# Moving convolutions and operand sums within VectorE's order in a two-layer decoder trunk

## The chip, the cores and the metric

The kernel runs on one core of a Trainium2 chip. Time is device time in microseconds of one execution, the median of three runs. The core's engines work side by side, each through its own instructions in a fixed order: TensorE (PE; PEld is its weight load), VectorE (DVE), ScalarE (ACT), GpSimd (POOL), and SyncE (SP), which here only issues loads. An instruction that waits holds up everything behind it on its engine.

## The reference, cut to what matters

A trunk of two layers over 256 tokens of width 2048: a gated linear attention layer, then an attention layer that reads a shared K/V, each followed by a gated feed-forward part with a convolution. The change touches the feed-forward parts:

```python
def conv_ffn(x, norm_w, w_up, conv_w, conv_b, w_down):
    h = rms_norm(x, norm_w) @ w_up                # (256, 2 * 5632)
    hp = jnp.pad(h, ((0, 0), (CONV_WIDTH - 1, 0), (0, 0)))
    acc = conv_b
    for j in range(CONV_WIDTH):                   # 3 taps back in time
        acc = acc + conv_w[j] * hp[:, j:j + S]
    a, u = jnp.split(acc, 2, axis=-1)
    return (jax.nn.silu(a) * u) @ w_down          # (256, 2048)
```

All is float32, and every matrix product is as exact as that asks for.

## The kernel before

**Weight pieces.** Weights are read once, in raw tiles of 128 x 2048 (three buffers, `wraw`, loaded by SyncE at L96). Each tile is used in pieces of 1024 columns or fewer. For each piece ScalarE rounds a high part (`whi`, L140) and VectorE subtracts it to get the low part (`wlo`, L141); three TensorE products of high and low parts (of weights and of activations, split likewise) give one product in full precision. High and low pieces have three buffers each, with some every fourth piece in a larger pool, so both engines work only a few pieces ahead of TensorE. `step()` marks the passing of one piece; `after(n, job)` puts a job n pieces later in the program. A tile scheduler then fixes each engine's order; it may pull an instruction forward unless `issue_after` ties it behind another. `ws.behind()` ties what stands in its scope behind the casts of the latest piece.

**Up-projection.** `ffn` goes through 22 groups J of 8 pieces. Each group's result is transposed, stored and fetched in another layout (`store`, `load`, GpSimd's queue, into `upT`), and later `convolve` (L670 to L689) makes two column blocks j of the hidden activations `hid`: on ScalarE L676 twice, L684 and L303, on VectorE L680 twice, L682 twice, L685 and L304. Group J's two convolutions were due 7 and 9 pieces after its group ends, so group 20's fell into group 21 and into the start of the down projection, and group 21's into its places 6 and 1+.

**Down projection.** `down` goes twice (b = 0, 1; half of the output columns each) through the 22 pairs of hidden blocks, in an order written by hand: for `dn0`, and for the first half of `dn1`, `0 2 4 6 1+ 8 3+ 10 5+ 12 7+ 14 9+ 16 11+ 17 13+ 18 15+ | 19 20 21` (in `dn0`'s second half 19 stands ahead of the bar). I call each entry a place. A plain place has two pieces and 24 matmuls (8 products). A place with a plus ("seven") gets along with seven products, 21 matmuls in four pieces, for sums of operands: VectorE makes sums of the raw weights (`t`, L106 to L108) and splits them too, and the activations' sums `comb` come from `combine` (L603 to L606, then a split at L303 and L304). Pairs 1, 3, 5, 7 are summed during the up-projection (`EARLY`); 9, 11, 13, 15, and 17 in the second half of `dn1`, by `combine_parts` (L613, then `combine`), written two places ahead of use, but with nothing that ties them there. The places behind the bar, the tail, are gone through twice, once for each half of the columns; behind the body's last seven place, L754 to L758 join the seven products and GpSimd adds the residual from memory (L760), and L769 adds the tail's sums.

Of the kernel before, what the change touches and what calls it, by code (L numbers as in the profile page):

```python
# [27 lines left out]
FT = F // 128  # L28
# [9 lines left out]
def _order(text):  # L38
# [3 lines left out]


EARLY = (1, 3, 5, 7)
ORDERS = {
    "go": [_order("0 1+ 2 3+ 4 | 5 6 7"), _order("0 2 1+ 3+ 4 | 5 6 7")],
    "dn0": [_order("0 2 4 6 1+ 8 3+ 10 5+ 12 7+ 14 9+ 16 11+ 17 13+ 18 15+ | 19 20 21"),
# [110 lines left out]
def trunk(ctx: ExitStack, tc: tile.TileContext, xT, x_tok, cst, msk, w1p, w2a, w_k, w_qa, w_v2, w_v, w_g, w_go,  # L158
# [27 lines left out]
    ws = WeightStream(tc, raw, parts)  # L186
# [4 lines left out]
    for w, groups, cols in plan:  # L191
        if cols is None:
            for g, order in enumerate(ORDERS[groups]):
                ws.add_quads(w, g, order, groups in ("go", "mo"))
# [74 lines left out]
    def after(steps, job):  # L269
        later.append((cur[0] + steps, job))  # L270
# [28 lines left out]
    def rows(xs):  # L299
        return lambda kt: xs[kt // 2][:, kt % 2, :]  # L300
# [54 lines left out]
    xs = rows(nrm.xs)  # L355
# [255 lines left out]
    def combine_parts(k, xs, into):  # L611
        t = temp("whole")
        V.tensor_add(t, xs[k][:, :, :S], xs[k][:, :, S:])  # L613
        combine(k, [(t[:, i, :128], t[:, i, 128:]) for i in range(2)], into)

    def sevens(name):
        return {k for order, _ in ORDERS[name] for k, seven in order if seven}

# [25 lines left out]
    def ffn(layer, nrm, then):  # L644
        xs = rows(nrm.xs)
        hid, sums = [], {}
        whole = [None, None]
        cw = C_CW + layer * 3 * 2 * FT
        cb = C_CB + layer * 2 * FT
        turned = dram.tile([FT // 2, 16, 32, 4, 64], F32, name=f"turned{layer}")  # L650

        def square(ps):
            z = slot([128, 16, 2, 32], F32, "z")
            for t in range(2):
                tok = temp("tok", (128, 512))
                A.activation(tok, ps[:, t, :], AF.Copy, scale=nrm.woven[:, t:t + 1])
                V.transpose(z[:, :, t, :], tok.rearrange("p (a b) -> p a b", b=32))  # L657
            return z

        def store(J, z):  # L660
            nc.gpsimd.dma_start(turned[J].rearrange("(a i) r q c -> (i r) a (q c)", a=4),  # L661
                              z.rearrange("p (a q) t c -> p a (q t c)", a=4))

        def load(J):
            f = slot([128, 4, S], F32, "upT")
            for q in range(4):
                nc.gpsimd.dma_start(f[32 * q:32 * q + 32].rearrange("p a (i c) -> p (a i) c", i=4),  # L667
                                  turned[J][:, :, q, :].rearrange("a r c -> r a c"))
            return f

        def convolve(j, t):
            au = temp("au")
            with ws.behind():
                for i in range(2):
                    n = i * FT + j
                    A.activation(au[:, i, :], t[:, i, :], AF.Identity, bias=col(cb + n),  # L676
                                 scale=col(cw + 2 * 2 * FT + n))
            for i in range(2):
                n = i * FT + j
                V.scalar_tensor_tensor(au[:, i, 1:], t[:, i, :S - 1], col(cw + 2 * FT + n), au[:, i, 1:],  # L680
                                       op0=OP.mult, op1=OP.add)
                V.scalar_tensor_tensor(au[:, i, 2:], t[:, i, :S - 2], col(cw + n), au[:, i, 2:],  # L682
                                       op0=OP.mult, op1=OP.add)
            A.activation(au[:, 0, :], au[:, 0, :], AF.Silu)  # L684
            V.tensor_mul(au[:, 0, :], au[:, 0, :], au[:, 1, :])  # L685
            if j % 2 == 0:
                hid.append(slot([128, 2, 2 * S], F32R, "hid"))
            split(hid[-1][:, j % 2, :S], hid[-1][:, j % 2, S:], au[:, 0, :])
            whole[j % 2] = (au[:, 0, :128], au[:, 0, 128:])  # L689
            if j % 2 and j // 2 in EARLY:  # L690
                combine(j // 2, whole, sums)

        f = {}
        for J in range(FT // 2):
            z = gemm_tok(xs, 1, square)
            after(1, lambda J=J, z=z: store(J, z))
            after(2, lambda J=J: f.update({J: load(J)}))
            for i in range(2):
                after(7 + 2 * i, lambda J=J, i=i: convolve(2 * J + i, f[J][:, 2 * i:2 * i + 2, :]))
        then(hid, sums)  # L700

    def down(name, xs, combos, res, done, jobs):

        for b, (order, n_tail) in enumerate(ORDERS[name]):
            new = [k for k, seven in order if seven and k not in combos]
            todo = {i: list(js) for i, js in jobs.get(b, {}).items()}
            for k in new:
                at = next(i for i, (k_, _) in enumerate(order) if k_ == k)
                todo.setdefault(max(at - 2, 0), []).append(lambda k=k: combine_parts(k, xs, combos))
            low = acc_ps.tile([128, 2, 512], F32, name="acc")  # L710
            p = {2: low[:, 0], 3: low[:, 1], 4: bank("p4", (128, 512)), 8: bank("p8", (128, 512))}
            left = dict.fromkeys(range(1, 9), 0)
            for k, seven in order:
                for n in ((1, 5, 7, 6, 4, 3, 2) if seven else (2, 3, 4, 8, 2, 3, 4, 8)):
                    left[n] += 3
            begun = set()

            def prods(*todo):

                w = step()  # L720
                for n, _, _ in todo:
                    if n not in p:
                        two = acc_ps.tile([128, 2, 512], F32, name="acc")
                        p.update({n: two[:, 0], {1: 6, 5: 7}[n]: two[:, 1]})
                for xi, wi in ((0, 0), (1, 0), (0, 1)):
                    for n, x, f in todo:
                        left[n] -= 1
                        T.matmul(p[n], x[xi], w[wi][:, 512 * f:512 * f + 512], start=n not in begun, stop=left[n] == 0)  # L728
                        begun.add(n)

            def part(k, i, t):
                x = xs[k][:, i, 128 * t:]
                return x[:, :128], x[:, S:S + 128]

            def comb(k, f):
                return combos[k][:, f, 0], combos[k][:, f, 1]

            last = max(i for i, (k, seven) in enumerate(order) if seven)
            for i, (k, seven) in enumerate(order[:-n_tail]):
                for job in todo.get(i, ()):  # L740
                    job()
                if seven:
                    prods((1, part(k, 0, 0), 0))
                    prods((3, comb(k, 3), 0), (2, part(k, 1, 0), 1))
                    prods((5, comb(k, 0), 0), (7, comb(k, 2), 1))
                    prods((6, comb(k, 1), 0), (4, part(k, 1, 1), 1))
                else:
                    for a in range(2):
                        prods(*((n, part(k, a, t), f)
                                for n, t, f in ((2, 0, a), (3, 0, 1 - a), (4, 1, a), (8, 1, 1 - a))))  # L750
                if i == last:

                    r = [temp(f"c{n}", (128, 512)) for n in range(4)]
                    A.copy(r[0], p[1])  # L754
                    V.tensor_add(r[1], r[0], p[6])  # L755
                    V.tensor_add(r[2], r[1], p[7])
                    V.tensor_add(r[1], r[1], p[5])
                    V.tensor_add(r[3], r[2], p[5])  # L758
                    for n in (0, 2, 1, 3):
                        nc.gpsimd.dma_start(r[n], res(n // 2, 2 * b + n % 2), accum_op=OP.add)  # L760
            for f, ns in enumerate(((2, 4), (3, 8))):
                for i, (k, _) in enumerate(order[-n_tail:]):
                    for job in todo.get((f, i), ()):
                        job()
                    prods(*((n, part(k, a, t), a) for a in range(2) for t, n in enumerate(ns)))
                if f:
                    ws.prefetch(cur[0])
                for t, n in enumerate(ns):
                    V.tensor_add(r[2 * t + f], r[2 * t + f], p[n])  # L769
                    done(t, 2 * b + f, r[2 * t + f])  # L770
# [212 lines left out]
    xs = rows(n_q.xs)  # L983
    for g in range(4):
# [4 lines left out]
        f = (q8[:, g % 2 * 4:g % 2 * 4 + 4], (q1[:, 0:2], q1[:, 2:4]))  # L989
        qf.append(f)  # L990
        head_through(g, z, [(11, lambda x, f=f: features(x, f, 1.0, 1))])
    xs = rows(xkv)
    for g in range(4):
# [3 lines left out]
        f = (k8[:, g % 2 * 4:g % 2 * 4 + 4], [slot([128, 2, 2, S], F32R, f"k1{c}") for c in range(2)])  # L997
# [120 lines left out]
```

## Time and profile before

| | us |
|---|---|
| runs (device time) | 2194.74, 2199.5, 2194.8; median 2194.8 |
| profiled execution, device time | 2194.64 |
| its span, first to last instruction | 2192.9 |
| mean granted TensorE clock | 0.998 |
| up-projection of layer 1 ends, body of `dn0` begins | 866.42 |
| tail of `dn0`'s first half begins | 969.24 |
| body of `dn1` begins, its tail begins | 1954.61, 2057.02 |

How to read it: busy times are sums over an engine's instructions within the span; the chain that ended last is followed back from the last instruction to whatever released it. The averages cover stages with different limits, so each stage has to be read from its own stretch.

### The profile page before, as it was taken

Reading aid. Unit: us, or ns where it says so; the run is one execution under the profiler, and the core shown is the slowest. Engines: PE = TensorE matmul, PEld = TensorE weight load, DVE = VectorE, ACT = ScalarE, POOL = GpSimd, SP = SyncE. Lnnn points to the kernel's source line nnn. Section 1 sums busy time; section 2 is a strip of 40 time slices with the busy share of each in tenths; the row PEclk is TensorE's granted clock in tenths of the full one; section 3 lists DMA queues with packets and bytes.
Section 4 is the critical chain, followed back from the end, with each engine's and each line's share of the span. In section 5 each row is a group of like instructions: output and inputs, shape, how many; then the busy total and the mean of one; then the engine's idle time right before and its main releaser. Section 6 shows DMA issues by size and latency. Waiting matters only on the chain.

```text
span 2192.9 us, 26952 instructions
## 1 busy us (share of the span) xinstructions
PE 2171.7 (99%) x9693; PEld 1793.4 (82%) x9693; DVE 1593.7 (73%) x2190; ACT 1283.0 (59%) x1856; POOL 301.1 (14%) x448
## 2 busy tenths in 40 slices
PE   9999999999999999999999999999999999999999
PEld 7888887888888888788888888888888888887887
DVE  5655586667776767887857787676777676779886
ACT  6545665556565656556556676555656565556554
POOL 1011111111111111000013242011111111110000
PEclk9999999999999999999999999999999999999999
DMA  8465577576777777566577787576677777774655
GB/s 306 177 234 208 186 244 251 206 247 230 239 249 249 241 239 242 180 235 237 210 258 261 271 279 229 205 235 230 233 248 237 248 235 249 236 242 186 231 209 173
DMA packets 92104, 510.11 MB, mean 233 GB/s; under 512 B 13713, under 2 KB 14753, under 8 KB 41922
## 3 DMA queue, kind: packets, MB, share of 16 engines
q1 hardware_dynamic: 60578, 417.53, 53.9%
q0 software_dynamic: 30816, 90.28, 15.3%
q8 instruction: 76, 1.25, 0.2%
q10 hardware_dynamic: 576, 0.58, 0.1%
q14 instruction: 58, 0.48, 0.1%
HBM read 463.22 MB, written 45.11 MB: 232 GB/s over the span
## 4 chain that ended last, share of the span: by engine, by line
PE 86%; issue 10%; DMA 3%; DVE 1%; ACT 0%; POOL 0%; SPq 0%; ACTq 0%; POOLq 0%; DVEq 0%
PE acc L290 45%; PE acc L293 22%; PE acc L728 10%; PE p L728 6%; DMA wraw<-w_go 1%; DMA c<-rows 1%; ACT whi L140 0%; PE sT L561 0%; PE o L578 0%; DMA wraw<-w_v 0%; DVE wlo L141 0%; PE acc L793 0%; PE s L910 0%; POOL upT L667 0%; DMA gn<-cst 0%
## 5 line engine op out<-in xcount | busy, mean ns | idle before, releaser
L141 DVE TENSOR_TENSOR wlo<-wraw,whi 128x1024 fp32r<-128x1024 f32 (+1 forms) x786 | 930.0, 1191 | 423.2 <-ACT whi L140 401.1
L140 ACT CAST whi<-wraw 128x1024 fp32r<-128x1024 f32 (+1 forms) x786 | 798.6, 1026 | 639.7 <-PE acc L290 415.8
L290 PE MATMUL acc<-whi,xw 128*128 128x512 f32 x3840 | 953.6, 390 | 3.5 <-ACT whi L140 2.6
L290 PEld LDWEIGHTS acc<-whi,xw 128*128 128x128 f32 x3840 | 720.7, 188 | 154.8 <-ACT whi L140 3.0
L293 PE MATMUL acc<-wlo,xw 128*128 128x512 f32 x1920 | 514.5, 389 | 0.0
L293 PEld LDWEIGHTS acc<-wlo,xw 128*128 128x128 f32 x1920 | 360.2, 188 | 74.9
L728 PE MATMUL acc<-whi,hid 128*128 128x512 f32 x572 | 182.5, 391 | 3.6 <-DVE c L769 2.2
L728 PE MATMUL p<-whi,hid 128*128 128x512 f32 x506 | 166.3, 390 | 0.0
L667 POOL DMA_DIRECT2D upT<-turned x176 | 114.0, 654 | 147.8 <-DMA turned<-z 60.1
L140 ACT CAST whi<-t 128x1024 fp32r<-128x1024 f32 x82 | 85.5, 1051 | 77.1 <-PE p L728 43.3
L728 PEld LDWEIGHTS acc<-whi,hid 128*128 128x128 f32 x572 | 106.8, 188 | 27.7 <-DVE c L769 3.0
L290 PE MATMUL acc<-whi,xkv 128*128 128x512 f32 x512 | 128.8, 391 | 0.0
L661 POOL DMA_DIRECT2D turned<-z x44 | 34.0, 774 | 677.2 <-DVE z L657 614.8
L676 ACT ACTIVATE au<-upT,cs 128x256 f32<-128x256 f32 x176 | 96.0, 595 | 52.4 <-DMA upT<-turned 52.3
L728 PE MATMUL acc<-whi,comb 128*128 128x512 f32 x328 | 108.2, 394 | 5.7 <-ACT whi L140 5.6
L728 PEld LDWEIGHTS p<-whi,hid 128*128 128x128 f32 x506 | 94.8, 188 | 19.8
L290 PEld LDWEIGHTS acc<-whi,xkv 128*128 128x128 f32 x512 | 94.6, 188 | 18.7
L680 DVE SCALAR_TENSOR_TENSOR au<-upT,cs,au 128x255 f32<-128x255 f32 x176 | 77.2, 472 | 41.7 <-ACT au L676 41.6
L141 DVE TENSOR_TENSOR wlo<-t,whi 128x1024 fp32r<-128x1024 f32 x82 | 99.1, 1219 | 5.4 <-ACT whi L140 3.9
L728 PE MATMUL acc<-wlo,hid 128*128 128x512 f32 x286 | 94.8, 390 | 2.0 <-DVE wlo L141 2.0
L760 POOL DMA_DIRECT2D c<-rows x24 | 21.2, 1052 | 466.9 <-DVE c L755 454.9
L728 PE MATMUL p<-wlo,hid 128*128 128x512 f32 x253 | 83.6, 389 | 0.0
(251 smaller groups left out, 1950.5 us busy)
## 6 DMA issues: line engine op xcount, KB each, us to landing
wraw<-w_up SPq DMA_DIRECT2D x176, 1024.0 KB, 5.3
wraw<-w_dn SPq DMA_DIRECT2D x88, 1024.0 KB, 5.0
turned<-z POOLq DMA_DIRECT2D x44, 512.0 KB, 3.5
upT<-turned POOLq DMA_DIRECT2D x176, 128.0 KB, 4.9
wraw<-w_g SPq DMA_DIRECT2D x16, 1024.0 KB, 4.9
wraw<-w_go SPq DMA_DIRECT2D x16, 1024.0 KB, 6.3
wraw<-w_mq SPq DMA_DIRECT2D x16, 1024.0 KB, 5.3
wraw<-w_kk SPq DMA_DIRECT2D x16, 1024.0 KB, 6.2
```

The lines of the kernel that those rows point to most:

```text
L140: one = nc.scalar.copy(hi[:, a:b], src[:, a:b])
L141: two = nc.vector.tensor_sub(lo[:, a:b], src[:, a:b], hi[:, a:b].bitcast(F32))
L290: T.matmul(ps[:, t, :], xs(kt)[:, x0 + 128 * t:x0 + 128 * t + 128], hi[:, c:c + 512], start=kt == 0 and x0 == 0, stop=False)
L293: T.matmul(ps[:, t, :], xs(kt)[:, 128 * t:128 * t + 128], lo[:, c:c + 512], start=False, stop=kt == KT - 1)
L661: nc.gpsimd.dma_start(turned[J].rearrange("(a i) r q c -> (i r) a (q c)", a=4), z.rearrange("p (a q) t c -> p a (q t c)", a=4))
L667: nc.gpsimd.dma_start(f[32 * q:32 * q + 32].rearrange("p a (i c) -> p (a i) c", i=4), turned[J][:, :, q, :].rearrange("a r c -> r a c"))
L676: A.activation(au[:, i, :], t[:, i, :], AF.Identity, bias=col(cb + n), scale=col(cw + 2 * 2 * FT + n))
L680: V.scalar_tensor_tensor(au[:, i, 1:], t[:, i, :S - 1], col(cw + 2 * FT + n), au[:, i, 1:], op0=OP.mult, op1=OP.add)
L728: T.matmul(p[n], x[xi], w[wi][:, 512 * f:512 * f + 512], start=n not in begun, stop=left[n] == 0)
L760: nc.gpsimd.dma_start(r[n], res(n // 2, 2 * b + n % 2), accum_op=OP.add)
```

## The change

The four convolutions of the last two groups of each up-projection (J = 20, 21) are due 24 pieces later, at pieces 23, 25, 31 and 33 of the down projection: in its order at places 5+, 12, 14 and 9+. And `combine_parts` is now issued behind the latest piece's casts at the place where it is written, so that the scheduler can't pull the sums forward.

```diff
+LAST = (FT // 2 - 2, FT // 2 - 1)
...
             for i in range(2):
-                after(7 + 2 * i, lambda J=J, i=i: convolve(2 * J + i, f[J][:, 2 * i:2 * i + 2, :]))
+                after(7 + 2 * i + (24 if J in LAST else 0),
+                      lambda J=J, i=i: convolve(2 * J + i, f[J][:, 2 * i:2 * i + 2, :]))
...
     def down(name, xs, combos, res, done, jobs):
+
+        def parts_behind(k):
+            with ws.behind():
+                combine_parts(k, xs, combos)
...
-                todo.setdefault(max(at - 2, 0), []).append(lambda k=k: combine_parts(k, xs, combos))
+                todo.setdefault(max(at - 2, 0), []).append(lambda k=k: parts_behind(k))
```

The added lines move line numbers: L106, L141, L304, L603, L613 and L680 of before are L107, L142, L305, L604, L614 and L681 after, and L728 is L734. The orders of GpSimd and SyncE are the same before and after; ScalarE's moves with VectorE's.

VectorE before, at place 1+ of `dn0` (`t_7040`, `t_7041` are 1+'s weight sums, `t_7160` 3+'s; `au` is a convolution's work tile, `whole` a sum's):

```order
L141 TENSOR_TENSOR wlo<-t_7040,whi 128x1024
L685 TENSOR_TENSOR au<-au 128x256
L613 TENSOR_TENSOR whole<-hid 128x512
L304 TENSOR_TENSOR hid<-au,hid 128x256
L603 TENSOR_TENSOR comb<-whole 128x128
L605 TENSOR_TENSOR comb<-whole 128x128
L613 TENSOR_TENSOR whole<-hid 128x512
L141 TENSOR_TENSOR wlo<-t_7041,whi 128x1024
L106 TENSOR_TENSOR t_7160<-wraw 128x1024
L604 TENSOR_TENSOR comb<-comb,whole 128x128
```

VectorE after, at the same place (`t_7017`, `t_7018` are 1+'s sums, `t_7114`, `t_7115` 3+'s):

```order
L107 TENSOR_TENSOR t_7114<-wraw 128x1024
L142 TENSOR_TENSOR wlo<-t_7017,whi 128x1024
L108 TENSOR_TENSOR t_7115<-t_7114,wraw 128x512
L142 TENSOR_TENSOR wlo<-wraw,whi 128x1024
L109 TENSOR_TENSOR t_7115<-wraw,t_7115 128x512
L142 TENSOR_TENSOR wlo<-wraw,whi 128x1024 x2
```

Convolutions and sums have left this place; what remains is the work on weights.

VectorE before, around place 9+ (`t_7405`, `t_7406` are its weight sums):

```order
L106 TENSOR_TENSOR t_7405<-wraw 128x1024
L141 TENSOR_TENSOR wlo<-t_7318,whi 128x1024
L141 TENSOR_TENSOR wlo<-wraw,whi 128x1024
L107 TENSOR_TENSOR t_7406<-t_7405,wraw 128x512
L141 TENSOR_TENSOR wlo<-wraw,whi 128x512
L141 TENSOR_TENSOR wlo<-wraw,whi 128x1024 x2
L304 TENSOR_TENSOR comb<-comb 128x4x128
L108 TENSOR_TENSOR t_7406<-wraw,t_7406 128x512
```

VectorE after, around place 9+ (`t_7382`, `t_7383` are its weight sums):

```order
L142 TENSOR_TENSOR wlo<-wraw,whi 128x1024
L686 TENSOR_TENSOR au<-au 128x256
L107 TENSOR_TENSOR t_7382<-wraw 128x1024
L683 SCALAR_TENSOR_TENSOR au<-upT,cs,au 128x254
L305 TENSOR_TENSOR comb<-comb 128x4x128
L683 SCALAR_TENSOR_TENSOR au<-upT,cs,au 128x254
L305 TENSOR_TENSOR hid<-au,hid 128x256
L108 TENSOR_TENSOR t_7383<-t_7382,wraw 128x512
L142 TENSOR_TENSOR wlo<-t_7382,whi 128x1024
L614 TENSOR_TENSOR whole<-hid 128x512
```

Here convolutions and sums now stand between the operations on weights; from place 12 to 18 the order is of this kind.

TensorE before, in the tail of `dn0`'s first half (`acc_6974` and `p8_6976` collect this half's tail, `acc_7916` is the second half's first sum):

```order
L728 MATMUL p8_6976<-whi_7826,hid_7122 128x512 x4
L728 MATMUL p8_6976<-wlo_7827,hid_7122 128x512 x2
L728 MATMUL acc_7916<-whi_7852,hid_3444 128x512 x4
L728 MATMUL acc_6974<-whi_7792,hid_6763 128x512 x4
L728 MATMUL acc_6974<-wlo_7793,hid_6763 128x512 x2
```

TensorE after, at the same place (`acc_6974` and `p8_6976` are now `acc_6962` and `p8_6964`):

```order
L734 MATMUL p8_6964<-whi_7826,hid_7446 128x512 x4
L734 MATMUL p8_6964<-wlo_7827,hid_7446 128x512 x2
L734 MATMUL acc_7916<-whi_7852,hid_3444 128x512 x4
L734 MATMUL acc_7916<-wlo_7853,hid_3444 128x512 x2
L734 MATMUL acc_6962<-whi_7792,hid_6763 128x512 x4
```

Two matmuls of the second half now stand ahead of the four that follow on the same accumulator as the tail's first sums.

## The prediction

> **What bounds the kernel now.** First the page: engine shares and the chain that ended last.
>
> ```profile
> PE 2171.7 (99%) x9693; PEld 1793.4 (82%) x9693; DVE 1593.7 (73%) x2190; ACT 1283.0 (59%) x1856; POOL 301.1 (14%) x448
> PE 86%; issue 10%; DMA 3%; DVE 1%; ACT 0%; POOL 0%; SPq 0%; ACTq 0%; POOLq 0%; DVEq 0%
> ```
>
> TensorE sets the time nearly everywhere, and the change leaves its matmuls alone. So it can act only where TensorE stands still. Second, the stretches of the two down projections: "body" is the 19 places ahead of the tail in the first half of an order (places 0 to 15+ of `dn0`, then of `dn1`).
>
> ```profile
> 866.42:969.24 102.82, 99.79 (x433) 80.53 (x432) 94.25 (x127) 61.14 (x76) 3.37 (x5) 1.00 0.57 204
> 866.42:888.18 21.76, 21.76 (x97) 18.02 (x96) 16.65 (x25) 11.96 (x19) 3.37 (x5) 1.00 0.83 261
> 888.18:913.08 24.90, 21.93 (x91) 16.42 (x90) 24.90 (x44) 15.10 (x20) 0.00 (x0) 1.00 0.28 108
> 1017.42:1083.38 65.96, 65.96 (x292) 54.62 (x291) 58.19 (x61) 38.76 (x42) 0.54 (x1) 1.00 0.57 218
> 1954.61:2057.02 102.41, 99.47 (x434) 80.62 (x432) 94.28 (x127) 61.06 (x76) 3.36 (x5) 1.00 0.58 205
> ```
>
> The columns are the stretch, its length, then PE, PEld, DVE, ACT and POOL busy with counts, then granted clock, DMA share and GB/s. In the undisturbed fourth stretch 291 weight loads (one per matmul) take 65.96 us: 0.2267 us each. A body has 432, so it needs 432 x 0.2267 = 97.9 us. The first took 102.82, the second 102.41: TensorE stands still 4.9 and 4.5 us, **9.4 us in all**. The third stretch says why: places 1+ to 10, where VectorE (DVE) is busy without a gap, 24.90 of 24.90. Third, the waits there:
>
> ```profile
> 893.96 0.73 PE L728 MATMUL acc<-whi,hid 128*128 128x512 f32 x2 [0.74 <-ACT whi L140]
> 897.99 0.72 PE L728 MATMUL acc<-wlo,hid 128*128 128x512 f32 x2 [1.02 <-DVE wlo L141]
> ```
>
> VectorE owes TensorE the low halves of weight pieces, and the convolutions and operand sums stand between them.
>
> **What a convolution and a sum cost.** VectorE's own pitch, from rows where it never pauses (a row starts before the one ahead of it has ended):
>
> ```profile
> 888.24 0.87 DVE L682 SCALAR_TENSOR_TENSOR au<-upT,cs,au 128x254 f32<-128x254 f32 x2
> 889.03 1.22 DVE L141 TENSOR_TENSOR wlo<-t,whi 128x1024 fp32r<-128x1024 f32 x1
> ...
> 910.01 0.28 DVE L606 TENSOR_TENSOR comb<-whole,comb 128x128 f32<-128x128 f32 x1
> 910.21 0.68 DVE L141 TENSOR_TENSOR wlo<-wraw,whi 128x512 fp32r<-128x512 f32 x1
> 910.81 0.41 DVE L304 TENSOR_TENSOR hid<-au,hid 128x256 fp32r<-128x256 f32 x1
> 911.15 2.35 DVE L141 TENSOR_TENSOR wlo<-wraw,whi 128x1024 fp32r<-128x1024 f32 x2
> 913.42 0.68 DVE L108 TENSOR_TENSOR t<-wraw,t 128x512 f32<-128x512 f32 x1
> ```
>
> From start to start: 1.135 us for 1024 columns, 0.60 for 512, 0.34 for 256, 0.20 for 128, 0.40 for a multiply-add of L680 or L682. A convolution is 4 x 0.40 + 2 x 0.34 = 2.3 us, a sum 0.60 + 4 x 0.20 + 0.60 = 2.0. A plain place costs VectorE 2 x 1.135 = 2.3 us beside 24 matmuls (5.44 us); a seven place 4 x 1.135 + 3 x 0.60 = 6.3 us beside 21 (4.76 us). A pair of them leaves 10.2 - 8.6 = 1.6 us free.
>
> One rule speaks against these pitches. In the Trainium skill, "VectorE: DVE Perf Modes", section "The DRAIN you can't avoid", the next operation starts only when the pipe has emptied, though an operation that nothing holds starts earlier. By the first half each of some 73 operations in the sum below would cost its full duration, 0.08 us more, and each body would lose 5.8 us more; the 2.35 us above for two operations of 1.22 us bear out the second half, and I go by the pitch.
>
> **Part 1: what goes.** Four convolutions per layer leave the up-projection's end and places 0 to 10, and four sums stay at their places instead of gathering there. The 9.4 us have these as their cause and go. Nothing else is late there: SyncE's and GpSimd's orders are unchanged, and without the extras the four plain places at the front need 9.1 us of VectorE in 21.8. That cover is wasted, though, since casts wait for buffers that TensorE frees, so VectorE can't work ahead.
>
> **Part 2: where it lands.** In the new order everything stands between the second piece of place 12 and that of place 17, where seven and plain places alternate. Counted there for layer 0: 3 of L106, 3 each of L107 and L108, 17 low halves of 1024 columns and 4 of 512, four convolutions (16 multiply-adds, 8 of 256 columns), sums with 4 of 512, 12 of 128 and 3 splits of 512: 20 x 1.135 + (3 + 3 + 4 + 4 + 3) x 0.60 + 16 x 0.40 + 8 x 0.34 + 12 x 0.20 = 44.4 us. TensorE needs 144 matmuls there, 32.6 us. VectorE's lead at the start I take from the second half of `dn0`, which has the same places without extras:
>
> ```profile
> 1034.86 2.36 DVE L141 TENSOR_TENSOR wlo<-wraw,whi 128x1024 fp32r<-128x1024 f32 x2
> ...
> 1040.31 0.62 PE L728 MATMUL acc<-wlo,hid 128*128 128x512 f32 x2
> ```
>
> The first of the two is place 12's second piece: ready at 1034.86 + 1.22 = 1036.08, used at 1040.31, 4.2 us ahead. So TensorE waits 44.4 - 32.6 - 4.2 = **7.6 us** by place 17; layer 1's order has one L108 fewer ahead of that point, **7.0 us**. About 3.2 us of it fall at place 9+, the rest at 13+ and 17. Behind it VectorE catches up.
>
> **Part 3: tiles that land late.** A raw tile can be loaded only when the one three places before it is used up. The rows: the queue's issue behind place 12's last low half, the landings of the 16 loads from 900 to 975 us, and VectorE waiting for that load.
>
> ```profile
> 920.41 4.11 SPq L96 DMA_DIRECT2D wraw<-w_dn  x2
> ...
> DMA to landing us min/median/max: 4.6/4.8/7.1
> ...
> 926.75 1.23 DVE L106 TENSOR_TENSOR t<-wraw 128x1024 f32<-128x1024 f32 x1 [1.49 <-DMA wraw<-w_dn]
> ```
>
> Once VectorE has fallen behind, it then waits for DMA too, as it did here 1.49 us. In the new order 11+'s tile is loaded after 14's last low half and asked for 4.4 us later, its cast another 0.7 before the low half: 4.8 + 0.7 - 4.4 = 1.1 us. 15+'s is asked for 3.3 us after 17's, with some 1.5 us of slack by then: 2.2 - 1.5 = 0.7. Bounds per layer: 0 (all hidden) and, with landings of 7.1, about 5. I take 1.8 and 1.1 (layer 1 asks for the last tile later): 2.9 us.
>
> **Part 4: tail and the tenth sum.** At the end of the first half TensorE waits for the first addition of L769, which waits for a DMA:
>
> ```profile
> 983.36 0.96 PE L728 MATMUL acc<-whi,hid 128*128 128x512 f32 x3 [0.81 <-DVE c L769]
> 2071.69 1.19 PE L728 MATMUL acc<-whi,hid 128*128 128x512 f32 x4 [1.36 <-DVE c L769]
> ```
>
> The new order puts two more matmuls ahead of the waiting one and their low half ahead of L769: 2 x 0.23 us of each wait covered, -0.9 in all. The one sum that `dn1`'s second half needs leaves this spot for place 15, beside alternating places: between 0 and its 2.0 us, I take 0.3, as its split of 0.6 is there already.
>
> **Sum.** +7.6 + 7.0 + 2.9 - 9.4 - 0.9 + 0.3 = +7.5, say +8 us. The profiled execution took 2194.64 us (span 2192.9), the median of the three runs is 2194.8: no difference to speak of. Forecast **2202.5 us**. A measurement of this kernel tells 0.3%, 6.6 us, from no change: faster is below 2188.2, slower above 2201.4.
>
> **Rivals.**
> *The old waits go and no new one comes*: the slack of 1.6 us per pair and the lead carry the extras, so only part 1 and the tail count: 2194.6 - 9.4 - 0.9 = 2184.3. It decides at 12.2 us of extra work (five pairs and a lead of 4.2): 4 x 2.3 + 4 x 2.0 = 17.2 us of convolutions and sums stand there. To carry them VectorE would need a lead of 9 us. Chance 0.06.
> *About even*: the lead in each layer is 1.4 us longer than that row's and the landings are hidden: 14.6 - 2.8 - 9.4 - 0.6 = +1.8, 2196.4; from 2190 to 2200, as more or less of the new waits remains. For it speaks that 4.2 us is one row's lead, against it that no slack is left to lengthen it. Chance 0.26.
> *The clock drops.* Granted clock and first long wait:
>
> ```profile
> 10.00:20.00 10.00, 7.38 (x26) 5.59 (x25) 5.53 (x9) 6.35 (x11) 0.00 (x0) 0.83 1.02 402
> 892.00:910.00 18.00, 15.29 (x62) 11.26 (x63) 18.00 (x30) 10.98 (x15) 0.00 (x0) 1.00 0.31 117
> ...
> 14.28 4.38 PE L290 MATMUL acc<-whi,xw 128*128 128x512 f32 x11 [2.62 <-ACT whi L140]
> ```
>
> After a wait of 2.62 us 11 matmuls took 4.38 us instead of 2.5, and the clock of that stretch is 0.83; waits of about 1 us left it at 1.00. The new waits come in lumps of 3 to 4 us at 9+ and 13+. If each costs 1.8 us, four add 7 us: 2210. VectorE is behind then anyway, which hides part of it. Chance 0.16. The Trainium skill ("TensorE: Matmul & The Clock Gate", section "What's actually happening") has the clock halved after an idle window of about 3.4 us that runs freely; the row agrees that a wait shorter than this can be enough.
>
> **How the numbers follow.** Forecast case (2200 to 2206) 0.52, clock or late landings (2206 to 2214) 0.16, about even 0.26, faster 0.06. Slower by over 0.3%: 0.16 and four fifths of 0.52, nearly 0.6; the remainder of the forecast and nearly all of the even case are within it, 0.34; faster 0.06. The range 2195 to 2211 leaves out the fast case, the edge of the even one and of the upper one.
>
> **What would show it.** Right: no wait at places 1+ to 10, and VectorE without a gap from place 12 to 18 with TensorE waits on low halves at 9+, 13+ and 17, some 8 to 9 us per layer. Wrong: waits there under 5 us per layer (lead or pitch misjudged), or waits left at 1+ to 10 (they had another cause). A clock below 1.00 in these stretches would be the third rival.

## The result, and the profile after

The changed kernel took 2210.97 us (median of 6 runs, 2208.42 to 2213.32), the kernel before 2195.49 on the same chip (6 runs, 2192.91 to 2199.5): a ratio of 1.0068, 95% interval 1.0057 to 1.0080, so 12.5 to 17.6 us **slower**. The forecast was 2202.5, in a range from 2195 to 2211: the sign is right, the loss is about twice the one forecast, and the measured time lies at the very end of the range. The profiled execution took 2208.68 us.

The page of the changed kernel: span, engine shares, and the group of down-projection matmuls on weight sums (columns: busy, mean ns of one, idle before it and what ended it).

```profile
span 2206.9 us, 26941 instructions
...
PE 2177.2 (99%) x9693; PEld 1795.4 (81%) x9693; DVE 1597.0 (72%) x2190; ACT 1283.5 (58%) x1856; POOL 301.9 (14%) x448
...
L734 PE MATMUL acc<-whi,comb 128*128 128x512 f32 x328 | 108.8, 397 | 16.1 <-ACT whi L141 16.0
```

Busy times are nearly those of before; the loss is waiting, most of it ahead of one kind of matmul, the high half of a weight sum times an operand sum. TensorE's waits for high and for low halves over the whole span (us in total, times, longest), before and after:

```profile
PE acc L728 <- ACT whi L140: 7.1, 7, 3.7
...
PE acc L728 <- DVE wlo L141: 2.5, 4, 1.0
```

```profile
PE acc L734 <- ACT whi L141: 16.0, 9, 3.9
...
PE acc L734 <- DVE wlo L142: 1.2, 3, 0.5
```

The longest of each, 3.7 and 3.9 us, stands at some 350 us, far ahead of the bodies. In the two bodies the waits for high halves grew from 1.7 and 1.7 us to 6.4 and 5.5, and those for low halves fell from 1.3 and 1.2 us to 0 and 1.0. So high halves already made more than half of the old waits. (The list counts from the modelled end of a matmul, so it shows less than a body loses: 2.50 us where starts lie 2.89 apart, below.)

The stretches (columns as in the prediction): the body of `dn0`, its places 1+ to 10, the stretch from 14 to 13+, and the body of `dn1`.

```profile
868.61:977.42 108.81, 102.45 (x433) 82.88 (x432) 95.56 (x128) 61.23 (x77) 3.38 (x5) 0.97 0.54 193
890.37:910.77 20.40, 20.40 (x92) 16.90 (x90) 16.72 (x18) 11.38 (x12) 0.00 (x0) 1.00 0.50 180
925.73:967.22 41.49, 35.13 (x136) 27.12 (x135) 38.41 (x63) 22.04 (x32) 0.00 (x0) 0.92 0.39 146
1963.01:2069.89 106.88, 100.35 (x434) 80.31 (x432) 94.93 (x127) 61.26 (x77) 3.38 (x5) 1.00 0.52 194
```

Less 97.93 us (432 x 0.2267), the bodies hold 10.9 and 8.95 us in which TensorE stands still or runs slowly, where 4.9 and 4.5 were. Places 1+ to 10 take 90 x 0.2267 = 20.40 us: nothing is left of the old waits. In the first body the granted clock is 0.97, in the second 1.00. TensorE's timeline at the same spot of both bodies (start, us, instruction, matmuls in the group, idle before):

```profile
928.90 0.39 PE L734 MATMUL acc<-wlo,hid 128*128 128x512 f32 x1
931.79 1.45 PE L734 MATMUL acc<-whi,comb 128*128 128x512 f32 x4 [2.50 <-ACT whi L141]
933.03 1.05 PE L734 MATMUL acc<-whi,hid 128*128 128x512 f32 x2
...
936.72 0.62 PE L734 MATMUL acc<-wlo,hid 128*128 128x512 f32 x2
...
2023.31 0.39 PE L734 MATMUL acc<-wlo,hid 128*128 128x512 f32 x1
2026.20 1.21 PE L734 MATMUL acc<-whi,comb 128*128 128x512 f32 x4 [2.50 <-ACT whi L141]
2027.24 0.65 PE L734 MATMUL acc<-whi,hid 128*128 128x512 f32 x2
```

The wait is the same, 2.89 us from start to start. In the first body two matmuls behind it take 1.05 us, up to 936, and in the second 0.65: in the first the clock halved (granted 0.50 from 932.61 to 936.01), in the second it didn't. It halved a second time in the first body, after a wait of 3.25 us that ended at 958.64. What held the high half up, from VectorE's and ScalarE's timelines:

```profile
929.03 0.41 DVE L686 TENSOR_TENSOR au<-au 128x256 f32<-128x256 f32 x1
929.37 1.21 DVE L107 TENSOR_TENSOR t<-wraw 128x1024 f32<-128x1024 f32 x1
...
930.69 1.04 ACT L141 CAST whi<-t 128x1024 fp32r<-128x1024 f32 x1 [0.81 <-DVE t L107]
```

VectorE ends a convolution (L686), then makes the weight sum of 9+ (L107), ScalarE rounds it, and TensorE goes on at 931.79. The tail, where the prediction saw a gain of 0.9 us:

```profile
992.10 1.20 PE L734 MATMUL acc<-whi,hid 128*128 128x512 f32 x4 [0.91 <-DVE c L775]
...
2087.25 0.69 DVE L775 TENSOR_TENSOR c<-c,p 128x512 f32<-128x512 f32 x1 [2.40 <-DMA c<-rows]
...
2089.92 0.73 PE L734 MATMUL p<-whi,hid 128*128 128x512 f32 x2 [0.96 <-DVE c L775]
```

In layer 0 the wait is what it was. In layer 1 the one at 2071.69 has gone to 2089.92: VectorE waits for the residual's transfer, in order, and TensorE behind it. Those transfers start later: VectorE makes two low halves between the body's first join (L761) and the others, where it made one before, and GpSimd's last three transfers of the body start 8.0 us behind the body's end (2077.88) and not 6.65 (2063.67).

TensorE's own order moved too. Before, 9+'s first sum product stood behind the second piece of place 14 (`whi_7420`; `hid_5898` is 14's pair, `hid_5033` and `comb_7395` are 9+'s):

```
L728 MATMUL acc_7145<-whi_7432,hid_5033 128x512 x2
...
L728 MATMUL acc_6974<-whi_7420,hid_5898 128x512 x2
...
L728 MATMUL acc_7145<-wlo_7433,hid_5033 128x512
L728 MATMUL acc_7181<-whi_7460,comb_7395 128x512 x4
```

After, it stands ahead of that piece (`whi_7397`; 9+'s sums are `comb_7372`):

```
L734 MATMUL acc_7110<-whi_7409,hid_5033 128x512 x2
...
L734 MATMUL acc_7110<-wlo_7410,hid_5033 128x512
L734 MATMUL acc_7135<-whi_7449,comb_7372 128x512 x4
L734 MATMUL acc_6962<-whi_7397,hid_5898 128x512 x2
```

From the body's start (counted from 0) it is matmul 267 instead of 275, and at 13+ 357 instead of 368: asked for 1.8 and 2.5 us earlier (8 and 11 x 0.2267). The two longest waits of each body stand at these matmuls or at 334 (11+'s).

### The profile page after: what moved, and what is told of

Same layout as the page of the kernel before. It is cut to its first block, busy times and chain, and to the rows that moved or that the text cites. A ratio compares the mean times of both kernels' runs of the same rounds, so it can differ in the third digit from the quotient of the medians.

```text
span 2206.9 us, 26941 instructions
## 1 busy us (share of the span) xinstructions
PE 2177.2 (99%) x9693; PEld 1795.4 (81%) x9693; DVE 1597.0 (72%) x2190; ACT 1283.5 (58%) x1856; POOL 301.9 (14%) x448
## 4 chain that ended last, share of the span: by engine, by line
PE 84%; issue 10%; DMA 3%; DVE 2%; ACT 1%; POOL 0%; SPq 0%; DVEq 0%; ACTq 0%; POOLq 0%
PE acc L291 45%; PE acc L294 22%; PE acc L734 9%; PE p L734 6%; DMA wraw<-w_go 1%; DMA c<-rows 1%; DVE wlo L142 1%; ACT whi L141 1%; PE sT L562 0%; PE o L579 0%; DMA wraw<-w_v 0%; PE acc L799 0%; DMA wraw<-w_dn 0%; PE s L916 0%; DMA wraw<-w_mo 0%
## 5 line engine op out<-in xcount | busy, mean ns | idle before, releaser
L142 DVE TENSOR_TENSOR wlo<-wraw,whi 128x1024 fp32r<-128x1024 f32 (+1 forms) x786 | 930.6, 1191 | 459.9 <-ACT whi L141 442.6
L141 ACT CAST whi<-wraw 128x1024 fp32r<-128x1024 f32 (+1 forms) x786 | 800.5, 1027 | 692.4 <-PE acc L291 447.2
L734 PE MATMUL acc<-whi,hid 128*128 128x512 f32 x572 | 185.1, 393 | 0.9 <-DVE c L775 0.9
L734 PE MATMUL p<-whi,hid 128*128 128x512 f32 x506 | 167.9, 393 | 1.0 <-DVE c L775 1.0
L141 ACT CAST whi<-t 128x1024 fp32r<-128x1024 f32 x82 | 85.7, 1051 | 75.8 <-PE p L734 47.5
L734 PEld LDWEIGHTS acc<-whi,hid 128*128 128x128 f32 x572 | 107.7, 189 | 24.4 <-DVE c L775 1.7
L734 PE MATMUL acc<-whi,comb 128*128 128x512 f32 x328 | 108.8, 397 | 16.1 <-ACT whi L141 16.0
L734 PEld LDWEIGHTS p<-whi,hid 128*128 128x128 f32 x506 | 95.9, 190 | 21.8 <-DVE c L775 1.9
L142 DVE TENSOR_TENSOR wlo<-t,whi 128x1024 fp32r<-128x1024 f32 x82 | 99.4, 1220 | 11.6 <-ACT whi L141 9.9
L734 PE MATMUL acc<-wlo,hid 128*128 128x512 f32 x286 | 95.5, 390 | 1.1 <-DVE wlo L142 1.0
L734 PEld LDWEIGHTS acc<-whi,comb 128*128 128x128 f32 x328 | 61.8, 190 | 33.5 <-ACT whi L141 20.7
L734 PE MATMUL p<-wlo,hid 128*128 128x512 f32 x253 | 84.1, 390 | 0.0
```

The lines of the kernel that those rows point to most:

```text
L141: one = nc.scalar.copy(hi[:, a:b], src[:, a:b])
L142: two = nc.vector.tensor_sub(lo[:, a:b], src[:, a:b], hi[:, a:b].bitcast(F32))
```

## The experiments

**The same kernel again.**

> The changed kernel once more, for a second profile. If the later start of its first body (868.61 against 866.42 us) is only what differs between executions, the start lies anywhere from 866 to 871 here, and the bodies have 9 to 11 us of waits each as in the first profile; if it belongs to the change, 868.6 or later. If the clock halves only now and then, the count of halved stretches in the two bodies (two in layer 0, none in layer 1 in the first profile) is another one here. Time 2208 to 2213.

2210.8 us (2207.56 to 2213.71) beside 2198.08: ratio 1.006, interval 1.0042 to 1.0078. Its bodies:

```profile
867.43:976.29 108.86, 102.48 (x434) 82.86 (x432) 95.59 (x128) 61.26 (x77) 3.38 (x5) 0.97 0.53 193
1964.89:2071.86 106.97, 100.33 (x433) 80.31 (x432) 94.85 (x127) 61.26 (x77) 3.38 (x5) 1.00 0.53 193
```

Waits and halvings stand where they stood. The first body starts 1.2 us earlier, so its start differs between executions; one kernel below started its first body at 873.27 in one profile and at 869.14 in the other. Up to there each engine's instructions stand in the same order before and after. Whether the change has a part in the later start is still open: at some 322 us TensorE waits 0.6 to 1.8 us for `go`, in the thirteen profiles of the other kernels and not in the one of before, and the raw tiles of `w_go` land later in them (median 6.4 to 7.3 us against 6.3). No run shows why.

**Each part alone.** Convolutions back, sums still held:

```diff
-                after(7 + 2 * i + (24 if J in LAST else 0),
+                after(7 + 2 * i + 0,
```

> The changed kernel with its four convolutions per layer back where they were, so that only the sums are held back. Theory A (VectorE's throughput decides, place by place): work of VectorE in its order from place 2 to place 10 is 35.6 us against 36.7 us of matmuls, and from 12 to 13+ 42.8 against 40.8 with a lead of some 4 us, so almost no wait in either stretch: the old 9.4 us go and nothing comes, 2186 to 2189 us. Theory B (ScalarE's casts of weights stand behind its halves of convolutions, which wait for VectorE): the convolutions at places 2 to 10 still cost about half of the old waits, 2 to 2.5 us per layer: about 2191. Theory C (the old waits are the convolutions' alone): 2195, as before.

2200.7 us beside 2197.2: ratio 1.0009, interval 0.9995 to 1.0022. That is theory C's number but not its mechanism, and theory A missed by some 10 us. The bodies have 4.3 and 5.9 us of waits, of which the old ones at 1+ and 8 make up only 0.8 and 1.2, although the convolutions stand where they stood. The largest is new, at 13+'s first sum product, which in this order too is matmul 357, ahead of the second piece of 17. TensorE there, in layer 0 and in layer 1:

```profile
949.64 0.39 PE L734 MATMUL acc<-wlo,hid 128*128 128x512 f32 x1
952.07 1.20 PE L734 MATMUL acc<-whi,comb 128*128 128x512 f32 x4 [2.05 <-ACT whi L141]
...
2039.71 1.59 PE L734 MATMUL acc<-whi,comb 128*128 128x512 f32 x4 [2.05 <-ACT whi L141]
2041.10 1.05 PE L734 MATMUL acc<-whi,hid 128*128 128x512 f32 x2
```

By sums of work VectorE had room, but TensorE asked for the weight sum while VectorE was still on the low halves and sums ahead of it. And the same wait of 2.4 us halved the clock in layer 1 but not in layer 0: place 17 lost 3.69 us with it and 2.37 without, so a halving costs 1.3 us here.

Sums free, convolutions late:

```diff
-                todo.setdefault(max(at - 2, 0), []).append(lambda k=k: parts_behind(k))
+                todo.setdefault(max(at - 2, 0), []).append(lambda k=k: combine_parts(k, xs, combos))
```

> The changed kernel with its sums free again, so that only the convolutions come later. In the order the sums then gather behind the convolutions, from place 7+ on. Theory A: VectorE has 41.4 us of work from 7+ to 17 against 30.6 us of matmuls, with a lead of 4.2 us: 6.6 us of waits per layer, no less than with both parts, and the clock halves after the longest of them (2 us each): 2205 to 2212. Rival: the freed sums fill VectorE's idle time at places 0 to 10 and half of the new waits go: 2196 to 2200.

2207.91 us, ratio 1.0039 (1.0023 to 1.0055), as theory A said.

```profile
870.78:978.46 107.68, 101.88 (x433) 81.59 (x432) 96.32 (x129) 62.01 (x78) 3.37 (x5) 0.98 0.55 195
1963.83:2069.65 105.82, 100.57 (x434) 80.39 (x432) 95.84 (x129) 61.19 (x78) 3.37 (x5) 1.00 0.56 198
```

9.75 and 7.9 us of waits, nearly those of both parts: the late convolutions make the loss, with the sums in the same stretch. The sums, free to move, gathered behind them. Here the waits for low halves are the larger part (4.6 and 2.8 us in the list of waits, against 1.2 and 2.5 for high halves), as the prediction had it for the change. And the clock halved in the first body (granted 0.53 from 946.70 to 950.20) after 1.44 us between two starts, 0.8 us behind a gap of 1.1.

**The sums left out.**

```diff
         def parts_behind(k):
-            with ws.behind():
-                combine_parts(k, xs, combos)
+            combos[k] = combos[EARLY[-1]]
```

> The changed kernel with the operand sums of pairs 9, 11, 13, 15 (and 17) left out: the sums of pair 7 are used in their place, so that part of the result is another. It takes 2.0 us of VectorE and 0.6 us of ScalarE per sum away, four sums per layer, and leaves the later convolutions. Theory A: 7.6 us of waits less 6.6 us of work leaves about 1 us per layer, and no wait is long enough for the clock to drop: 2190 to 2194. Theory B (round trips of the convolutions between ScalarE and VectorE): the waits of about 3 us at 9+ and 2 us at 11+ stay: 2197 to 2201.

2190.21 us, ratio 0.9957 (0.9941 to 0.9973).

```profile
867.45:966.48 99.03, 98.25 (x433) 81.00 (x432) 88.04 (x105) 59.87 (x74) 3.37 (x5) 1.00 0.60 212
1952.90:2053.09 100.19, 98.94 (x434) 80.77 (x432) 88.01 (x105) 59.80 (x74) 3.37 (x5) 1.00 0.59 209
```

With 7.5 and 6.9 us less for VectorE (88.0 busy against 95.6 and 94.9) the bodies wait 1.1 and 2.26 us instead of 10.9 and 8.95, with the convolutions as late as ever. That is theory A's number (the kernel uses pair 7's sums in their place, so its result is another); the 3 and 2 us that theory B kept are not there. It also takes casts off ScalarE, and TensorE's order has the sum products at 275 and 364 again. That order alone doesn't take the waits away, as the kernel with the sums on GpSimd shows below.

**More for VectorE, less for ScalarE.** The high parts of the last convolutions and of the sums, cast by VectorE:

```diff
-        split(c[:, :, 0], c[:, :, 1], t)
+        (cast or A.copy)(c[:, :, 0], t)
+        V.tensor_sub(c[:, :, 1], t, c[:, :, 0].bitcast(F32))
...
-        combine(k, [(t[:, i, :128], t[:, i, 128:]) for i in range(2)], into)
+        combine(k, [(t[:, i, :128], t[:, i, 128:]) for i in range(2)], into, V.tensor_copy)
...
+            if j // 2 in LAST:
+                V.tensor_copy(hid[-1][:, j % 2, :S], au[:, 0, :])
+                V.tensor_sub(hid[-1][:, j % 2, S:], au[:, 0, :], hid[-1][:, j % 2, :S].bitcast(F32))
```

> The changed kernel with the high parts of the last four convolutions and of the sums of the down projection cast by VectorE and no longer by ScalarE. That adds 4 x 0.34 + 4 x 0.60 = 3.8 us of VectorE per layer (half of it if such a cast runs faster there) and takes the same eight casts off ScalarE, behind which casts of weights stand. Theory A: every us more on VectorE is a us more of waiting, 2214 to 2219. Theory B: ScalarE no longer waits for VectorE's last operation of a sum or a convolution (2.9, 1.6, 2.7 us in the profile of the changed kernel), and 3 to 6 us of waits go in all: 2205 to 2208.

2213.62 us, ratio 1.0071 (1.0054 to 1.0088). The two new groups on VectorE, and the bodies:

```profile
L609 DVE CAST comb<-comb 128x512 fp32r<-128x512 f32 x4 | 1.7, 425 | 0.1
L691 DVE CAST hid<-au 128x256 fp32r<-128x256 f32 x4 | 1.2, 290 | 0.0
```

```profile
867.57:977.18 109.61, 102.17 (x433) 82.78 (x432) 98.24 (x136) 57.23 (x69) 3.37 (x5) 0.97 0.54 192
1963.05:2072.42 109.37, 102.09 (x433) 83.11 (x432) 98.39 (x136) 57.95 (x69) 3.37 (x5) 0.97 0.53 192
```

VectorE has 2.7 and 3.5 us more to do, ScalarE 4.0 and 3.3 less, and TensorE waits 0.8 and 2.5 us longer. That is less than theory A's us for us, and layer 1's share may be the clock, which is 0.97 there now. Theory B, which had 3 to 6 us go, falls. A smaller gain from ScalarE's relief could hide behind VectorE's extra work; this run can't tell.

**The sums on GpSimd.** In the changed kernel, and with the convolutions as before and the sums written three places ahead of use:

```diff
-        V.tensor_add(t, xs[k][:, :, :S], xs[k][:, :, S:])
-        combine(k, [(t[:, i, :128], t[:, i, 128:]) for i in range(2)], into)
+        G.tensor_tensor(t, xs[k][:, :, :S].bitcast(F32), xs[k][:, :, S:].bitcast(F32), op=OP.add)
...
+        G.tensor_copy(c[:, :, 0], t)
+        G.tensor_tensor(c[:, :, 1], t, c[:, :, 0].bitcast(F32), op=OP.subtract)
```

> The changed kernel with the operand sums of the down projection (five additions and the split) made by GpSimd and not by VectorE and ScalarE. Theory A (what VectorE has to do between place 12 and 17 decides): as with the sums left out, 1 to 2.5 us of waits per layer, 2188 to 2192. Rival: a sum on GpSimd takes longer than its two places (about 10 us) or slows VectorE's own operations beside it, so that TensorE waits for sums or low halves as long as now: 2200 to 2212.

> Convolutions where they were before the change, and the sums made by GpSimd, written three places ahead of use and held there. Theory A: VectorE's work from place 2 to 10 is 35.6 us against 36.7, and behind that it has several us of slack; waits at 1+ and 8 of about 1 us per layer stay (0.8 and 1.2 with the sums held back on VectorE), the others go: 2186 to 2190, faster than both kernels. Rival: GpSimd too slow or in VectorE's way: 2197 or more.

2211.84 us (1.0071, interval 1.0052 to 1.0091) and 2213.43 (1.0067, 1.0048 to 1.0086): the rival, both times. The body of `dn0` in the changed kernel with the sums on GpSimd, and VectorE's weight sums and multiply-adds in it:

```profile
867.84:979.33 111.49, 102.78 (x433) 80.99 (x432) 99.67 (x105) 59.60 (x74) 43.95 (x33) 0.98 0.53 188
```

```profile
L107 DVE TENSOR_TENSOR t<-wraw 128x1024 f32<-128x1024 f32 x8 | 12.8, 1606 | 4.3 <-DMA wraw<-w_dn 4.3
...
L693 DVE SCALAR_TENSOR_TENSOR au<-upT,cs,au 128x254 f32<-128x254 f32 x8 | 7.1, 912 | 0.0
```

The same two groups with the sums left out:

```profile
L107 DVE TENSOR_TENSOR t<-wraw 128x1024 f32<-128x1024 f32 x8 | 9.8, 1221 | 1.0 <-DMA wraw<-w_dn 1.0
...
L683 DVE SCALAR_TENSOR_TENSOR au<-upT,cs,au 128x254 f32<-128x254 f32 x8 | 3.6, 480 | 0.0
```

1606 ns against 1221, and 912 against 480, the two groups that changed most: beside GpSimd's work VectorE's takes longer. VectorE is busy 99.67 us there, against 88.04 with the sums left out and 95.56 with the sums on it. The Trainium skill ("SBUF — State Buffer", section "Who interferes with whom") says that VectorE's operation on two tensors in SBUF contends with GpSimd's reads; these rows agree.

That body waits 13.6 us, though TensorE's sum products stand at 275 and 365, nearly as with the sums left out: so what took the waits away there was not TensorE's order alone. In the second kernel only 4.8 us of the profile's loss stand in the bodies (7.3 and 6.9 us of waits); 13 us stand in the tails, where TensorE waits for L785, the additions that were L769, and the clock halves behind these waits.

**11+'s tile sooner.**

```diff
+    for i, (w, g, c0, n) in enumerate(ws.chunks):
+        if (w is w_dn0 or w is w_dn1) and g == 0 and c0 // 2048 in (14,):
+            ws.cuts[i] = ((0, 512), (512, 2048))
```

> The changed kernel with the load of 11+'s raw tile, in both layers, cut in two: its first 512 columns, then the other 1536. VectorE's order stays as it is. If the late landing of this tile costs TensorE what the prediction's third part says (1.1 us per layer; ScalarE waits 2.37 and 2.28 us for it in the changed kernel's profile), ScalarE's wait falls by 1 to 2 us and the waits at 11+ and 17 by about 1 us per layer: 2207 to 2209. If VectorE's work alone decides and the idle time there is made good later, or the weight sums, which need 1536 columns, then wait in its place, nothing moves: 2210 to 2212.

2210.03 us, ratio 1.0055 (1.0036 to 1.0073): no difference from the changed kernel that can be told. ScalarE's wait for that tile in the changed kernel, in layer 0 and 1:

```profile
940.66 0.62 ACT L141 CAST whi<-wraw 128x512 fp32r<-128x512 f32 x1 [2.37 <-DMA wraw<-w_dn]
...
2034.98 0.62 ACT L141 CAST whi<-wraw 128x512 fp32r<-128x512 f32 x1 [2.28 <-DMA wraw<-w_dn]
```

With the load cut:

```profile
939.68 0.62 ACT L141 CAST whi<-wraw 128x512 fp32r<-128x512 f32 x1 [1.38 <-DMA wraw<-w_dn]
...
2036.01 0.62 ACT L141 CAST whi<-wraw 128x512 fp32r<-128x512 f32 x1 [4.65 <-DMA wraw<-w_dn]
```

In layer 0 the wait fell by 1 us and the body with it (9.9 us of waits instead of 10.9); in layer 1 it grew, and the clock halved at 14 as well (9.6 instead of 8.95). Inconclusive: about 1 us in the one layer in which the wait got shorter.

**Weight sums a piece earlier**, in the changed kernel and with the sums five places ahead (below):

```diff
-            for c_, _, kind_ in self.halves[n:n + (5 if n in self.deep else 3)]:
+            for c_, _, kind_ in self.halves[n:n + (5 if n in self.deep else 4)]:
```

> The changed kernel with the weight sums of a seven place begun one piece earlier in the program. Theory D: TensorE's long waits are for high halves of weight sums, which go from VectorE over ScalarE to TensorE and so fall due about 1.5 us ahead of a low half; a piece earlier (1.2 us) takes about 1 us off each of the two long waits per layer: 2205 to 2207. Theory A alone: VectorE has as much to do between 12 and 17 as before, and what the high halves gain the low halves lose: 2209 to 2213.

> Convolutions where they were before the change, operand sums held back five places ahead of use, and the weight sums begun one piece earlier. Beside the run with sums five places ahead (0.9989 of the kernel before, waits of 3.9 and 2.8 us in its bodies, the 2 us at 12, 7+, 16 and 11+ for high halves of weight sums). Theory D: those 2 us go and about 1 us at 1+ and 8 stays: ratio 0.997, some 6 us less than before. Rival: raw tiles are not there a piece earlier, so VectorE waits for loads and nothing is gained: ratio 0.999 to 1.001.

2217.1 us (1.0085, 1.0067 to 1.0103) and 2206.02 (1.0043, 1.0023 to 1.0062): worse both times, so theory D, which had time gained, falls. The changed kernel's bodies with it:

```profile
869.22:978.25 109.03, 102.94 (x433) 82.81 (x432) 95.47 (x128) 61.07 (x77) 3.37 (x5) 0.97 0.54 193
1967.53:2076.09 108.56, 101.89 (x433) 81.52 (x432) 95.52 (x128) 61.12 (x78) 3.37 (x5) 0.98 0.54 193
```

11.1 and 10.6 us. Its waits, in the same list as above:

```profile
PE acc L734 <- ACT whi L141: 11.2, 7, 4.1
PE acc L734 <- DVE wlo L142: 8.1, 10, 1.4
```

Those for high halves fell from 16.0 to 11.2 us (some 4 us of each stand ahead of the bodies), as D asked, but those for low halves rose from 1.2 to 8.1: here VectorE was not early for both.

**Convolutions as before, sums five places ahead.**

```diff
-                after(7 + 2 * i + (24 if J in LAST else 0),
+                after(7 + 2 * i + 0,
...
-                todo.setdefault(max(at - 2, 0), []).append(lambda k=k: parts_behind(k))
+                todo.setdefault(max(at - 5, 0), []).append(lambda k=k: parts_behind(k))
```

> Convolutions where they were before the change, and the sums on VectorE, held back but written five places ahead of use and not two. With two, TensorE waited 2.4 and 3.7 us at place 17, where a sum, the weight sums of 13+ and three low halves meet in VectorE's order. Theory A: with the sums at 5+, 12, 9+ and 16 the work of no two neighbouring places exceeds TensorE's by more than the lead; the waits at 9+ and 17 go (3.0 and 4.4 us) and 1 us per layer stays at 1+ and 8: 2190 to 2194. Rival: VectorE has no room anywhere in these 100 us (94 us busy), and the waits only move: 2197 to 2201.

> The kernel with convolutions as before the change and operand sums held back five places ahead of use, once more, to tell whether it beats the kernel before. From the bodies of its first profile (3.9 and 2.8 us of waits against 4.9 and 4.5) it should be 2.7 us faster: ratio 0.9988. If 1.71 us at 1+ in layer 0 (0.63 in layer 1) was a single event, that wait is 0.6 in both layers here.

2197.28 us beside 2198.08 (0.9989, 0.9974 to 1.0003), then 2192.48 beside 2195.77 (0.9981, 0.9967 to 0.9994). The bodies of the second profile:

```profile
869.14:969.02 99.88, 99.28 (x434) 80.70 (x433) 93.65 (x127) 60.70 (x76) 3.38 (x5) 1.00 0.60 210
1954.84:2054.61 99.77, 99.22 (x434) 80.76 (x432) 93.65 (x127) 60.70 (x76) 3.36 (x5) 1.00 0.60 210
```

1.95 and 1.85 us of waits (3.9 and 2.8 in the first profile, with one of 1.71 at 1+ that is not here). By the ratios to before it beats the changed kernel by 0.8 to 0.9%, and the one before by 0.1 to 0.2%, less than hoped: it is the better by the second interval, and by the first it may be level. Its TensorE order has the sum products behind the plain pieces, at 275 and 365, and the wait of sums held two places ahead, at 357, is gone. Whether the five places or TensorE's order brings that was not tried apart, since the scheduler sets the one by the other.

## Why the prediction was right in kind and short in size

The measured 2210.97 us lie 0.03 us inside the range, in the part that the prediction gave to the clock and to late landings (2206 to 2214, chance 0.16) and not in its forecast case (2200 to 2206, 0.52). The way the time would move was understood; that the range held it owes something to luck.

The sum of the prediction beside the two profiles, against the profile of before (us; a body is its length less 97.93):

| step | forecast | first | second |
|---|---|---|---|
| start of the first body | 0 | +2.2 | +1.0 |
| old waits gone | -9.4 | -9.4 | -9.4 |
| new waits, body of `dn0` | 7.6 + 1.8 = 9.4 | 10.9 | 10.9 |
| new waits, body of `dn1` | 7.0 + 1.1 = 8.1 | 8.95 | 9.0 |
| from `dn0`'s body to `dn1`'s | -0.45 | +0.2 | +3.2 |
| behind `dn1`'s body | -0.15 | +1.1 | +2.0 |
| sum | +7.5 | +14.0 | +16.8 |

**Part 1, right.** Both bodies have no wait at places 1+ to 10, so the convolutions and sums had caused all of them. Moving either alone took away all or most of them: none is left with the convolutions late, 0.8 and 1.2 us with the sums held back.

**Part 2, right in place and nearly in size.** The waits begin where the balance of work turns negative, between 14 and 9+, and end at 13+. From place 14 to 17 VectorE is without a gap, as forecast, but for 1.4 us in layer 0 and 1.3 in layer 1, where it waits for high halves while ScalarE waits for 11+'s raw tile. In layer 1, where the clock stayed up, they come to 8.95 us, against 8.1 forecast with the late tiles. Taking the sums away brings the waits down by 9.8 and 6.7 us for 7.5 and 6.9 us of work. Wrong was which operand TensorE would wait for: "low halves" it said, and it is the high half of a weight sum, 11.9 us against 1.0 in the two bodies. The waits of before were of both kinds, 3.4 us for high halves and 2.5 for low ones. One reason for the shift is a step that the prediction left out when it said that the change "leaves its matmuls alone": their number stays, their order doesn't. In a stretch that VectorE bounds, that should move waits rather than add any; no run shows the order alone. With the sums alone held back VectorE had room, and a wait of 2.4 us stood at the matmul that had moved; the balance of work did not see it, and my expectation for that kernel failed on it.

**The clock, the rival given 0.16, came true in part, on top of the forecast case.** The two lumps of layer 0 (2.9 and 3.25 us, as forecast 3 to 4) halved the clock for 7 or 8 matmuls each, in both profiles, and the lumps of layer 1 didn't. At the 1.3 us that a halving cost at place 17 with the sums alone, layer 0's two are 2.6 us; without them its 10.9 us would be 8.3, beside 9.4 forecast. That is an estimate, with a price from another kernel. By it the forecast case was nearly right for the bodies, 8.3 + 8.95 against 17.5, and their error was to set the clock beside it as another case and not as an added term. That the two agree so well is in part chance, as 2.9 of the 17.5 us are for late tiles. The Trainium skill ("TensorE: Matmul & The Clock Gate", section "What's actually happening") lets the clock fall after an idle window of about 3.4 us that runs freely. The free running fits what is seen, the same wait with and without a halving; the length doesn't, since 2.4 us were enough, and with the convolutions alone late 1.44 us behind a gap of 1.1.

**Part 3, right in kind.** 11+'s tile lands late: ScalarE waits 2.4 and 2.3 us for it. For 15+ no wait shows. That the first costs 1.1 us per layer is borne out in layer 0 alone.

**Part 4, wrong.** The 0.9 us did not come. Behind `dn0`'s body the wait for L775 is 1.1 us as before (2.6 with a halving in the second profile); behind `dn1`'s it turned from 1.5 us into several, 1.1 and 2.0 us more in all. It waits for a transfer of the residual, which starts when VectorE has joined the body's products. VectorE came to that later: behind `dn0`'s body it began 4.1 us after the body's end (981.51) and not 3.2 (972.46 behind 969.24). So the two matmuls put ahead only moved the wait. The step that failed took VectorE's time there as unchanged. The kernel with sums alone held back shows the same waits behind `dn1`, so the late convolutions aren't needed for them.

Whether the later start of the first body is the change's is open. What the medians have beyond the bodies' 10.5 us, 2 to 5 us, I can place in that start, in the tails and in more halvings, but only from these two profiles.

## What to carry to other kernels

Where a second engine feeds the first with no slack on average, add up its work from the spot where it is last ahead to the spot where it catches up, in its own order: that gave the waits here to about 1 us per layer, the clock's part taken off. Then look at whether the bound engine's order moved with the change, and which of its operands passes over two engines, since a wait stands there even where the balance of work has room. And where waiting comes in lumps of some 2 to 3 us, as here, add the clock to the sum, as a term and not as an alternative.

## What the runs showed of the chip that was not expected

- The clock halved after waits of some 2.4 us and more, and three times in the bodies after 1.4 to 1.8 us behind a gap of 0.7 to 1.1, but not each time: after 2.4 us in layer 1 and not in layer 0 of one execution, after 2.89 in layer 0 and not in layer 1 of another, after 1.44 in layer 0 and not after 1.43 in layer 1 of a third. In the bodies it stayed low for 5 to 8 matmuls, 0.43 us apart instead of 0.2267.
- VectorE was slower beside GpSimd's sums: multiply-adds of 254 columns took 912 ns on average, and 480 without them. Four casts of 512 columns took GpSimd 4.7 us in one kernel and 11.4 in the other, for a cause that was not looked for, where VectorE took 1.7.
- VectorE casts 512 columns in 425 ns, where a subtraction of 512 takes it 680 to 690.
